# RWKV scan: the state product no longer waits for the copy of y from the other PSUM bank

## The chip, the cores and the metric

One core of one Trainium2 chip runs the whole program. The metric is the device time of one execution in microseconds; the number given for a kernel is the median over its runs.

## The reference

A decoder trunk of two layers on a sequence of 1024 tokens of width 1024, float32. Each layer normalises x, projects it with one wide input matrix and runs three token mixers beside each other: a pooling mixer, a retention mixer with 4 heads, and an RWKV-7 mixer with 8 heads of 64. Their outputs are gated, projected, merged by per-channel gates, projected once more and added to x. The part that matters here is the recurrence of RWKV-7, which carries a 64 x 64 state S for each head from token to token:

```
def step(S, inp):
    r_t, w_t, k_t, v_t, a_t, b_t = inp
    sa = einsum('bhvk,bhk->bhv', S, a_t)
    S = S * w_t[:, :, None, :] + sa[..., None] * b_t[:, :, None, :] + v_t[..., None] * k_t[:, :, None, :]
    return S, einsum('bhvk,bhk->bhv', S, r_t)
_, y = lax.scan(step, zeros, xs)
y = head_norm(y, RWKV_NORM_EPS) * ln_w + ln_b
```

## The kernel before, in words

**The wide work.** Everything that is a projection is done by one helper. The sequence lies along the free axis in two halves of 512 tokens. Every weight tile is split into a rounded part (wh, ScalarE) and a rest (wl, GpSimd), as are the activations (hhi and hlo), and three matmuls of 128 x 128 weights on 512 tokens (wh with hhi, wh with hlo, wl with hhi) stand for one exact product. They add up in one of three PSUM banks with the tag acc. A weight tile is 2 halves x 4 blocks x 3 products x 2 token halves = 48 such matmuls. This is what the groups acc<-hhi,wh, acc<-hhi,wl and acc<-hlo,wh in the profile are. `split` (L561 to L563) makes wh and wl, with three buffers for each.

**The side tasks.** The mixers are Python generators in lanes (norm, post, rwkv, mix, ada). After each three matmuls of the wide work, `pump` lets every lane advance whose due time has come on a clock that the kernel keeps by hand: `mmul` adds an estimate for each matmul, `settle` one for each operation of the other engines, and `wait(x)` gives the time until x is estimated to be there. So a step of a scan is spread between wide matmuls, and this fixes the order in which the program is written. In the first stretch (`manual_schedule`) this order is kept on the four compute engines. Behind it the compiler's list scheduler orders each engine's queue from that order and its own model of when an instruction's operands are ready, so an instruction that its model sees held back can be overtaken by later ones. The engines then run their queues in order.

**The scan.** `rwkv_task` handles two heads (128 channels) at a time, so there are four of them in a layer and eight in the program, one after the other. The tokens are taken in 16 chunks of 64. `prepare`, `scores`, `invert` and `states` make everything that doesn't depend on the state. Then the loop over c (L999 to L1042) does the following for each chunk:

- ScalarE scales the state with the chunk's decay into SP (L1007).
- TensorE multiplies the state with the chunk's rows of AR into cy (L1009). This is the **state product**, two<-S,AR in the profile. Rows 64 to 127 of its output go into the update, and rows 0 to 63 are the part of y that comes from the old state.
- VectorE adds AV and writes xst (L1010).
- Two small matmuls make ch from xst (L1016), VectorE copies it to Z (L1017), one matmul multiplies BKt with Z (L1019), and VectorE makes the new state of each head from that and SP (L1022, twice in a chunk, S in the profile).
- Two small matmuls add the chunk's own part onto rows 0 to 64 of cy (L1029, the **y products**, two<-Z,G in the profile).
- ScalarE copies rows 0 to 63 of cy to y (L1037, the **copy of y**).

A float32 matmul appears in the profile as two matmuls with two weight loads, so the y products of a chunk are four rows and the state product two.

**The shared tile.** cy is not a tile of its own. `two` is one PSUM tile of two banks, and `cyt()` hands out its halves in turn:

```
two = ps_c.tile([P, 2 * HF], F32, tag="two", name="two")
...
def cyt():
    turn[0] ^= 1
    return two[:, turn[0] * HF : (turn[0] + 1) * HF]
```

Two chunks that follow each other use different banks; chunk c and chunk c-2 use the same. Dependencies are found for the tile: the state product of chunk c, which writes one half, is held until the copy of y of chunk c-1 has read the other. `two` is also used by the preparation of the next pair of heads, for scores (L901), the inversion (L939, L945) and the small projections (L781).

Of the kernel before, what the change touches and what calls it, by code (L numbers as in the profile page):

```python
# [17 lines left out]
P = 128  # L18
# [78 lines left out]
def trunk_kernel(ctx, tc, xT, cvec, pos, vecs, consts, w_ada, w_all, pool_w, lora_w, out):  # L97
    nc = tc.nc
# [19 lines left out]
    def nm(s):  # L118
        uid[0] += 1
        return f"{s}_{uid[0]}"  # L120
# [24 lines left out]
    two = ps_c.tile([P, 2 * HF], F32, tag="two", name="two")  # L145
    turn = [0]
# [4 lines that stand above are left out]
# [4 lines left out]
    def r8(s):  # L155
        return rp.tile([P, 2048], F32, tag="r8", name=nm(s))
# [3 lines left out]
    o = CST["bone"]  # L160
# [175 lines left out]
    def settle():  # L336
        if seen[0] is None:
            return
        insts = nc.cur_bb.bb.instructions
        for j in range(seen[0], len(insts)):  # L340
            i = insts[j]
            e = i.engine
            if e not in idle_at and e != ET.PE and e != ET.SP:
                continue
            ins, outs = (
                [b for b in (getattr(x, "bass_ap", None) for x in y) if b is not None] for y in (i.ins, i.outs)
            )
            if not outs:
                continue
            t = max([ready.get(x.tensor.name, 0.0) for x in ins] + [0.0])  # L350
            base = t if any(x.space == PSUM for x in ins) else clock[0]
            if e == ET.PE:
                t = clock[0] + 280
            elif e != ET.SP:
                c = cost(i, e, ins, outs)
                idle_at[e] = max(idle_at[e], base) + c
                t = max(t + c, idle_at[e]) + 80
                for x in ins:
                    if x.space == PSUM:
                        ready[x.tensor.name] = max(ready.get(x.tensor.name, 0.0), t)  # L360
            for x in outs:
                ready[x.tensor.name] = t
        seen[0] = len(insts)

    def await_(out, *ins):
        names = [x.tensor.name for x in ins] + [behind.pop(out.tensor.name, "")]
        clock[0] = max(clock[0], *(ready.get(n, 0.0) for n in names))
# [14 lines left out]
    def wait(*aps, spare=0.0):  # L382
        settle()
        names = [x.tensor.name if hasattr(x, "tensor") else x.name for x in aps]
        t = max(ready.get(n, 0.0) for n in names) + spare
        if len(mxq) == 2:
            t = max(t, ready.get(mxq[0], 0.0) + 600)
        return max(0.0, t - clock[0])
# [43 lines left out]
    def add(k, task):  # L432
        if not lanes[k]:
            due[k] = clock[0]
        lanes[k].append(task)
        return task

    def mmul(out, lhsT, rhs, start=True, stop=True, timed=False, **kw):
        n = rhs.free_size()
        fast = rhs.dtype == F32R  # L440
        settle()
        await_(out, *(() if timed else (lhsT, rhs)))
        m = lhsT.free_size()
        clock[0] += (n + 32) / 2.4 if fast else 2 * max(n, 1.6 * m - 92, m - 16) * 0.875
        nc.tensor.matmul(out, lhsT=lhsT, rhs=rhs, start=start, stop=stop, **kw)  # L445

    def trans(out, in_, timed=False):
        settle()
# [99 lines left out]
    def mm1(ps, w, k, r, start, stop):  # L548
        (whi, wlo), (rh, rl) = w, r
        for j, (a, b) in enumerate(((whi, rh), (whi, rl), (wlo, rh))):  # L550
            mmul(ps, a[:, k * P : (k + 1) * P], b, start=(start and j == 0), stop=(stop and j == 2))
            pump()
# [139 lines left out]
    def layer_norm(y, n, w, eps, tile_, eng=nc.vector):  # L692
        y3 = y.rearrange("p (n w) -> p n w", w=w)
        mean = sp.tile([P, n], F32, tag="mn", name=nm("mn"))
        nc.vector.tensor_reduce(mean, y3, axis=mybir.AxisListType.X, op=ALU.add)
        nc.vector.tensor_scalar_mul(mean, mean, 1.0 / w)
        yc = tile_("yc")
        yc3 = yc.rearrange("p (n w) -> p n w", w=w)
        eng.tensor_tensor(
            yc3, y3, mean.unsqueeze(2).to_broadcast([P, n, w]), op=ALU.subtract  # L700
        )
        sq = tile_("ysq")
        nc.scalar.square(sq, yc)
        var = sp.tile([P, n], F32, tag="vr", name=nm("vr"))
        nc.vector.tensor_reduce(
            var, sq.rearrange("p (n w) -> p n w", w=w), axis=mybir.AxisListType.X, op=ALU.add
        )
        rsqrt(var, eps, 1.0 / w)
        eng.tensor_tensor(yc3, yc3, var.unsqueeze(2).to_broadcast([P, n, w]), op=ALU.mult)  # L709
        return yc  # L710
# [72 lines left out]
    def rwkv_task(l, hp, kT, rT, vp, lt, lw):  # L783
        hc = slice(hp * P, (hp + 1) * P)
        AR = r8("AR").rearrange("p (c j t) -> p c j t", j=2, t=CH)
# [11 lines left out]
        jt = lambda t, rows, c: t[rows, c, :, :].rearrange("p j t -> p (j t)")  # L797
# [118 lines left out]
        start = [0.0]  # L916
# [79 lines left out]
        for S in SS:  # L996
            nc.gpsimd.memset(S, 0.0)
        yield wait(MT, *SS)
        for c in range(16):  # L999
            par = c % 2  # L1000
            prog[(l, hp)] = c
            if c % 8 == 0:
                y = t_ri("y")
            S, Sn = SS[par], SS[1 - par]
            pcc = pc[:, c : c + 1]
            SP = sp.tile([P, P], F32, tag="SP", name=nm("SP"), bufs=1)
            nc.scalar.activation(SP, S, AF.Copy, scale=pcc)  # L1007
            cy = cyt()
            mmul(cy[:, 0:P], jt(AR, slice(0, P), c), S)  # L1009
            nc.vector.tensor_tensor(xst[0:64, :], cy[64:128, 0:P], AV[:, c * P : (c + 1) * P], op=ALU.add)  # L1010
            yield wait(xst)
            ch = ps_c.tile([P, HF], F32, tag="ch", name=nm("ch"))
            for hd in range(2):
                cols = slice(64 * hd, 64 * hd + 64)
                u0 = (16 * hd + c) * P
                mmul(ch[0:65, cols], Gf[:, u0 + 64 : u0 + 129], xst[:, cols])  # L1016
            nc.vector.tensor_copy(Z[0:64, c, :], ch[0:64, 0:P])  # L1017
            yield wait(Z)
            mmul(ch[:, P : 2 * P], BKt[:, c, :], Z[:, c, :])  # L1019
            for hd in range(2):  # L1020
                rw = slice(64 * hd, 64 * hd + 64)
                nc.vector.scalar_tensor_tensor(  # L1022
                    Sn[rw, rw], ch[rw, P + 64 * hd : P + 64 * hd + 64], pc[rw, c : c + 1], SP[rw, rw],
                    op0=ALU.mult, op1=ALU.add,
                )
            yield 500
            for hd in range(2):
                cols = slice(64 * hd, 64 * hd + 64)
                mmul(  # L1029
                    cy[0:65, cols],  # L1030
                    G[:, 16 * hd + c, 0:65],
                    Z[:, c, cols],
                    start=False,
                    skip_group_check=True,
                )
            o = (c % 8) // 2 * P
            nc.scalar.copy(y[64 * par : 64 * par + 64, o : o + P], cy[0:64, 0:P])  # L1037
            yield wait(Sn)
            if c % 8 == 7:
                h = c // 8  # L1040
                yn = layer_norm(y, 8, 64, RWKV_EPS, t_ri, nc.gpsimd)
                posts[l, hp, h] = add("post", rwkv_post(l, hp, h, yn, bvs[h]))  # L1042

    def rwkv_post(l, hp, h, yn, bv):
        yield 6500
        yield wait(yn, spare=3000)
        ps = mx("yt")
        for j in range(4):
            trans(ps[:, j * P : (j + 1) * P], yn[:, j * P : (j + 1) * P])
        ob = t_ri("wob")  # L1050
        nc.vector.scalar_tensor_tensor(ob, ps, vv(l, "ln_w", hp), bv, op0=ALU.mult, op1=ALU.add)
        nc.sync.dma_start(out=od[l][2, hp, h], in_=ob)
        yield 100
# [51 lines left out]
    def evac(item, ps, h):  # L1105
# [9 lines left out]
        elif kind in ("k", "r", "v"):  # L1115
# [8 lines left out]
            if kind == "v" and h == 1:  # L1124
                st[("task", i)] = rwkv_task(l, i, st[("k", i)], st[("r", i)], st[("v", i)], st["lt"], lw)
                add("rwkv", st[("task", i)])
# [279 lines left out]
    for l in range(L):  # L1406
# [94 lines left out]
        while wready[0][0][0] != "out":  # L1501
# [11 lines left out]
            else:  # L1513
# [6 lines left out]
                for d, h in dh:  # L1520
                    ps = acc_ps()
                    mm3(ps, ws[d - d0], [osplit[n][k][h] for k in range(4)], True, True)
                    o = (d % 2) * T + h * HF
# [28 lines left out]
        for part, (h, sl) in enumerate(parts):  # L1552
# [3 lines left out]
            for i, d in enumerate(out_order(l, part)):  # L1556
# [17 lines left out]
                for j in range(2):  # L1574
                    rhs = [[m[:, sl] for m in merged[k][h]] for k in range(4 * j, 4 * j + 4)]
# [129 lines left out]
```

## Time and profile before

| | us |
|---|---|
| runs | 2446.65, 2447.24, 2447.24 |
| median | 2447.24 |
| the profiled execution | 2443.31 |
| its span, first to last instruction | 2441.4 |
| mean granted clock of TensorE, share of full speed | 0.989 |
| TensorE busy | 2363.0 (97%) |
| VectorE busy | 1315.2 (54%) |
| GpSimd busy | 818.5 (34%) |
| ScalarE busy | 799.3 (33%) |

In the rows of the profile, PE is TensorE's matmuls, PEld its weight loads (which run beside the matmuls), DVE VectorE, ACT ScalarE, POOL GpSimd, SP SyncE, which issues the DMAs. "two<-S,AR" means that the tile two is written and S and AR are read. A row of the timeline gives the start in us from the begin of the span, the duration in us, engine, line and operation, and in brackets how long the engine had been idle and what ended that. L445 and L451 are the lines of the helpers through which all matmuls and transposes go, so they are told apart by their tiles. The ends of matmuls are modelled, their starts are recorded. In this trace the scans run in eight stretches, of which the first begins at 240 us and the last ends at 2099 us.

### The profile page before, as it was taken

The page shows a single profiled execution, that of the slowest core. Times are in us where ns is not written, and L with a number is a line of the kernel's source. Part 1 is how long each engine was busy: PE and PEld are TensorE (multiplying, and loading weights), DVE is VectorE, ACT ScalarE, POOL GpSimd, SP SyncE. Part 2 cuts the span into 40 slices and gives each one's busy share as a digit, 9 for nine tenths or more (in the row PEclk, how much of TensorE's full clock was granted, in tenths as well). Part 3 has the DMA queues.
Part 4 walks back from the last instruction along what each step waited for, and adds up shares of the span by engine and source line. Part 5 has one row for each costly group of instructions (what it writes and reads, how often), then busy time and mean ns, then how long its engine had stood idle before and what let it go on. Part 6 is the DMA issues. An engine that isn't in the chain of part 4 may idle for free. (4 is left out here: it accounts for less than half of the span.)

```text
span 2441.4 us, 34772 instructions
## 1 busy us (share of the span) xinstructions
PE 2363.0 (97%) x13312; PEld 1912.5 (78%) x13312; DVE 1315.2 (54%) x2564; ACT 799.3 (33%) x1481; POOL 818.5 (34%) x729
## 2 busy tenths in 40 slices
PE   5989999999999999999999999999999999999998
PEld 4768778778877878777877877887787888778888
DVE  7655477367458643457455646735644674322244
ACT  5542233333234222112354324323322322212243
POOL 4321232232232323374442222323313332455241
PEclk9999999999999999999999999999999999999999
DMA  7132112111213215666531211211111122543142
GB/s 251 49 109 70 40 40 75 44 48 46 70 54 109 75 61 165 191 211 194 162 118 44 79 40 40 80 39 44 63 61 40 62 75 73 183 129 97 54 151 79
DMA packets 122487, 220.52 MB, mean 90 GB/s; under 512 B 13904, under 2 KB 17232, under 8 KB 122320
## 3 DMA queue, kind: packets, MB, share of 16 engines
q1 hardware_dynamic: 122320, 218.29, 28.1%
q8 instruction: 105, 1.72, 0.3%
q14 instruction: 62, 0.51, 0.1%
HBM read 172.89 MB, written 45.35 MB: 89 GB/s over the span
## 5 line engine op out<-in xcount | busy, mean ns | idle before, releaser
L563 POOL TENSOR_TENSOR wl<-wr,wh 128x512 fp32r<-128x512 f32 x342 | 451.1, 1319 | 1161.1 <-ACT wh L562 1091.3
L445 PE MATMUL acc<-hhi,wh 128*128 128x512 f32 x2000 | 806.3, 403 | 7.8 <-ACT gsg L1140 6.6
L445 PE MATMUL acc<-hhi,wl 128*128 128x512 f32 x2000 | 809.2, 405 | 1.5 <-POOL r L1060 1.5
L445 PE MATMUL acc<-hlo,wh 128*128 128x512 f32 x2000 | 810.4, 405 | 0.0
L445 PEld LDWEIGHTS acc<-hhi,wh 128*128 128x128 f32 x2000 | 379.9, 190 | 76.3 <-ACT gsg L1140 7.9
L445 PEld LDWEIGHTS acc<-hhi,wl 128*128 128x128 f32 x2000 | 380.0, 190 | 67.9 <-POOL r L1060 2.0
L445 PEld LDWEIGHTS acc<-hlo,wh 128*128 128x128 f32 x2000 | 380.0, 190 | 64.7 <-issue 0.7
L562 ACT CAST wh<-wr 128x512 fp32r<-128x512 f32 x342 | 211.8, 620 | 629.6 <-PE acc L445 462.4
L445 PE MATMUL acc<-olo,wh 128*128 128x512 f32 x384 | 154.6, 404 | 5.9 <-POOL olo L563 5.9
L445 PE MATMUL acc<-oG,wh 128*128 128x512 f32 x384 | 154.3, 403 | 3.2 <-ACT oG L562 1.7
L445 PE MATMUL acc<-oG,wl 128*128 128x512 f32 x384 | 152.3, 398 | 0.0
L1010 DVE TENSOR_TENSOR xst<-two,MT 64x128 f32<-64x128 f32 x128 | 37.5, 293 | 182.2 <-PE two L445 181.4
L1022 DVE SCALAR_TENSOR_TENSOR S<-ch,pc,SP 64x64 f32<-64x64 f32 x256 | 72.5, 283 | 99.0 <-PE ch L445 96.2
L1007 ACT ACTIVATE SP<-S,pc 128x128 f32<-128x128 f32 x128 | 51.4, 402 | 213.1 <-DVE S L1022 202.8
L445 PEld LDWEIGHTS acc<-olo,wh 128*128 128x128 f32 x384 | 73.3, 191 | 24.8 <-POOL olo L563 8.6
L445 PEld LDWEIGHTS acc<-oG,wh 128*128 128x128 f32 x384 | 73.1, 191 | 23.3 <-ACT oG L562 2.9
L445 PEld LDWEIGHTS acc<-oG,wl 128*128 128x128 f32 x384 | 73.6, 192 | 17.6
L1529 DVE SCALAR_TENSOR_TENSOR gs<-gs,acc 128x512 f32<-128x512 f32 x64 | 43.5, 683 | 79.2 <-PE acc L445 79.2
L939 DVE TENSOR_TENSOR tm<-MT,two 64x30 f32<-64x30 f32 (+14 forms) x240 | 76.5, 319 | 12.9 <-ACT two L932 5.6
L945 DVE TENSOR_TENSOR two<-two,tm 64x30 f32<-64x30 f32 (+14 forms) x240 | 78.9, 329 | 7.3
L1527 DVE SCALAR_TENSOR_TENSOR mrg<-gs,acc 128x512 f32<-128x512 f32 x32 | 22.0, 686 | 107.6 <-PE acc L445 107.5
L1017 DVE COPY Z<-ch 64x128 f32<-64x128 f32 x128 | 36.0, 281 | 74.4 <-PE ch L445 73.9
(287 smaller groups left out, 3688.2 us busy)
## 6 DMA issues: line engine op xcount, KB each, us to landing
wr<-in_w_all SPq DMA_DIRECT2D x364, 256.0 KB, 2.6
gd<-gsg SPq DMA_DIRECT2D x74, 256.0 KB, 2.0
gs<-gd SPq DMA_DIRECT2D x74, 256.0 KB, 3.0
wada<-in_w_ada SPq DMA_DIRECT2D x70, 256.0 KB, 3.0
ol<-od SPq DMA_DIRECT2D x64, 256.0 KB, 2.9
ringG<-in_w_ada SPq DMA_DIRECT2D x26, 256.0 KB, 5.1
x<-in_xT SPq DMA_DIRECT2D x16, 256.0 KB, 4.9
od<-po SPq DMA_DIRECT2D x16, 256.0 KB, 2.0
```

The lines of the kernel that those rows point to most:

```text
L445: nc.tensor.matmul(out, lhsT=lhsT, rhs=rhs, start=start, stop=stop, **kw)
L562: nc.scalar.copy(hi, src)
L563: eng.tensor_tensor(lo, src, hi.bitcast(F32), op=ALU.subtract)
L939: nc.vector.tensor_tensor(pr, L3[:, i + 1 :, i : i + 1].to_broadcast([64, n, i]), M3[:, i : i + 1, 0:i].to_broadcast([64, n, i]), op=ALU.mult,
L945: nc.vector.tensor_tensor(M3[:, i + 1 :, 0:i], M3[:, i + 1 :, 0:i], pr, op=ALU.add)
L1007: nc.scalar.activation(SP, S, AF.Copy, scale=pcc)
L1010: nc.vector.tensor_tensor(xst[0:64, :], cy[64:128, 0:P], AV[:, c * P : (c + 1) * P], op=ALU.add)
L1017: nc.vector.tensor_copy(Z[0:64, c, :], ch[0:64, 0:P])
L1022: nc.vector.scalar_tensor_tensor(Sn[rw, rw], ch[rw, P + 64 * hd : P + 64 * hd + 64], pc[rw, c : c + 1], SP[rw, rw], op0=ALU.mult, op1=ALU.add,
L1527: nc.vector.scalar_tensor_tensor(m, s, 1.0, ps, op0=ALU.add, op1=ALU.mult)
L1529: nc.vector.scalar_tensor_tensor(s, s, 1.0, ps, op0=ALU.add, op1=ALU.mult)
```

## The change

`mmul` returns the instruction. The scan keeps the instructions of the copies of y in a list. For every chunk but the first it declares that the state product does not depend on the copy of the chunk before, and for every chunk from the third on it adds a dependency on the copy of the chunk before that, which read the same bank.

```diff
@@ mmul
-        nc.tensor.matmul(out, lhsT=lhsT, rhs=rhs, start=start, stop=stop, **kw)
+        return nc.tensor.matmul(out, lhsT=lhsT, rhs=rhs, start=start, stop=stop, **kw)
@@ rwkv_task
         yield wait(MT, *SS)
+        yout = []
         for c in range(16):
...
             cy = cyt()
-            mmul(cy[:, 0:P], jt(AR, slice(0, P), c), S)
+            sa = mmul(cy[:, 0:P], jt(AR, slice(0, P), c), S)
+            if c:
+                tc.declare_no_dep(sa.ins, yout[-1], reason="reads the other bank of two")
+            if c > 1:
+                tc.add_manual_dep(
+                    sa.ins,
+                    yout[-2].name,
+                    mybir.DependencyInfo(mybir.DependencyClass.Sync, mybir.DependencyReason.DATA),
+                    reason="read the same bank of two",
+                )
             nc.vector.tensor_tensor(xst[0:64, :], cy[64:128, 0:P], AV[:, c * P : (c + 1) * P], op=ALU.add)
...
             o = (c % 8) // 2 * P
-            nc.scalar.copy(y[64 * par : 64 * par + 64, o : o + P], cy[0:64, 0:P])
+            yout.append(nc.scalar.copy(y[64 * par : 64 * par + 64, o : o + P], cy[0:64, 0:P]).ins)
             yield wait(Sn)
```

## The prediction

> **What bounds the kernel now.** I read the page first: its busy times, its chain, its costliest group (behind the bar: busy time, mean ns of one, idle time before the group and what ended it).
>
> ```profile
> span 2441.4 us, 34772 instructions
> PE 2363.0 (97%) x13312; PEld 1912.5 (78%) x13312; DVE 1315.2 (54%) x2564; ACT 799.3 (33%) x1481; POOL 818.5 (34%) x729
> PE acc L445 13%; POOL olo L563 0%; PE ssps L445 0%; PE rbc L445 0%; DVE fin L627 0%; PE ch L445 0%; PE two L445 0%; DVE yc L709 0%; ACT wh L562 0%; POOL wl L563 0%; DVE xres L1577 0%; DVEq L1700 0%; DVE sq L1584 0%; PE yt L451 0%; PE rot L451 0%
> L445 PE MATMUL acc<-hhi,wh 128*128 128x512 f32 x2000 | 806.3, 403 | 7.8 <-ACT gsg L1140 6.6
> ```
>
> TensorE is busy 97% of the span, and what the chain could be followed through is nearly all wide matmuls into acc. What counts is how fast TensorE gets through its queue; a shorter chain of the scan is by itself worth nothing. Next, the busy time in the eight stretches in which the scan of one pair of heads runs (16 chunks each):
>
> ```profile
> core 0: us, PE busy (x) PEld busy (x) DVE busy (x) ACT busy (x) POOL busy (x), PEclk, DMA share, GB/s
> sum 604.00, PE 600.27 PEld 476.34 DVE 266.89 ACT 164.15 POOL 167.01; mean PE 75.03 PEld 59.54 DVE 33.36 ACT 20.52 POOL 20.88
> ```
>
> TensorE looks full there, 600 of 604 us. But the ends of matmuls are modelled, and a stretched matmul counts as busy, so time lost must be looked for in the starts. The waits of the weight loads, totals over the run, name a place:
>
> ```profile
> engine line waited for: us in total, times, longest us
> PEld two L445 <- ACT y L1037: 35.2, 98, 0.6
> PEld ch L445 <- DVE Z L1017: 8.9, 14, 1.7
> ```
>
> 98 of the 128 state products (two<-S,AR) load their weights late, behind the copy of y. The timeline shows one of them, an even chunk, in the order of time:
>
> ```profile
> 247.32 0.29 DVE L1022 SCALAR_TENSOR_TENSOR S<-ch,pc,SP 64x64 f32<-64x64 f32 x1
> 247.52 0.39 PE L445 MATMUL two<-Z,G 128*65 128x64 f32 x4
> 247.70 0.40 ACT L1007 ACTIVATE SP<-S,pc 128x128 f32<-128x128 f32 x1 [0.30 <-DVE S L1022]
> 247.72 0.48 PE L445 MATMUL acc<-hlo,wh 128*128 128x512 f32 x1
> 248.04 0.40 PE L445 MATMUL acc<-hhi,wl 128*128 128x512 f32 x1
> 248.13 0.26 ACT L1037 COPY y<-two 64x128 f32<-64x128 f32 x1
> 248.44 0.30 PEld L445 LDWEIGHTS two<-S,AR 128*128 128x128 f32 x2 [0.44 <-ACT y L1037]
> 248.44 0.49 PE L445 MATMUL two<-S,AR 128*128 128x128 f32 x2
> 248.69 0.48 PE L445 MATMUL acc<-hhi,wh 128*128 128x512 f32 x1
> ```
>
> The y products (two<-Z,G) are queued first, then two wide matmuls, then the state product. S was complete at 247.32 + 0.29 = 247.61. The copy of y ran behind the scaling of S on ScalarE and ended at 248.39, and the weights were loaded at 248.44, 0.05 later. An odd chunk, where the copy does not queue behind the scaling, and one in which the copy (at 252.07) was long done:
>
> ```profile
> 269.80 0.29 DVE L1022 SCALAR_TENSOR_TENSOR S<-ch,pc,SP 64x64 f32<-64x64 f32 x1
> 270.49 0.24 ACT L1037 COPY y<-two 64x128 f32<-64x128 f32 x1
> 270.51 0.40 PE L445 MATMUL acc<-hlo,wh 128*128 128x512 f32 x1
> 270.78 0.30 PEld L445 LDWEIGHTS two<-S,AR 128*128 128x128 f32 x2 [0.31 <-ACT y L1037]
> 271.03 0.47 PE L445 MATMUL acc<-hhi,wl 128*128 128x512 f32 x1
> ...
> 252.07 0.24 ACT L1037 COPY y<-two 64x128 f32<-64x128 f32 x1
> 252.57 0.39 PE L445 MATMUL acc<-hlo,wh 128*128 128x512 f32 x1
> 252.80 0.40 PE L445 MATMUL acc<-hhi,wl 128*128 128x512 f32 x1
> 252.80 0.42 PEld L445 LDWEIGHTS two<-S,AR 128*128 128x128 f32 x2
> 253.03 0.38 PE L445 MATMUL two<-S,AR 128*128 128x128 f32 x2
> 253.17 0.48 PE L445 MATMUL acc<-hhi,wh 128*128 128x512 f32 x1
> ```
>
> From the wide matmul before the state product to the one behind it takes 0.65 us in the even chunk (248.04 to 248.69), 0.52 in the odd one and 0.37 in the free one. So the waits cost TensorE 0.28 and 0.15 us, and each is 0.16 less than the idle time of the weight loads beside it (0.44, 0.31): the load is normally issued with the matmul ahead, and a start up to 0.16 late costs nothing.
>
> **The change part by part.** *Removed:* the wait of the state product of chunk c for the copy of chunk c-1. By the rows, 98 waits of 35.2 us in all, less 98 × 0.16 = 15.7 us that lay under the matmul ahead, are 19.5 us of TensorE. A few of the 98 only bear the copy's name, and in them S was late:
>
> ```profile
> 861.30 0.58 DVE L1022 SCALAR_TENSOR_TENSOR S<-ch,pc,SP 64x64 f32<-64x64 f32 x2
> 861.57 0.26 ACT L1037 COPY y<-two 64x128 f32<-64x128 f32 x1 [3.65 <-PE two L445]
> 861.66 0.40 PE L445 MATMUL acc<-hhi,wh 128*128 128x512 f32 x1
> 862.00 0.30 PEld L445 LDWEIGHTS two<-S,AR 128*128 128x128 f32 x2 [0.38 <-ACT y L1037]
> 862.25 0.48 PE L445 MATMUL acc<-hlo,wh 128*128 128x512 f32 x1
> ...
> 1843.32 0.30 PEld L445 LDWEIGHTS two<-S,AR 128*128 128x128 f32 x2 [0.39 <-ACT y L1037]
> ```
>
> Here the copy ended at 861.83, S at 861.88, and the load came 0.12 behind S: that is the shortest way from S to the load. The interval is 0.59, so 0.22 is lost and stays lost. There are four such (these are the first and the last): 0.9 us off, which leaves 18.6 us.
>
> *What is late next.* In the even chunk S would have let the load start at 247.61 + 0.12 = 247.73, and the latest start without loss is 248.04 + 0.16 = 248.20: 0.47 us to spare. In the odd one it is 270.21 against 270.67: 0.46. A wide matmul takes 0.23 (252.57 to 252.80), so S does not take the copy's place unless the product moves up by more than two of them.
>
> *Moved.* The queue of TensorE is ordered when the kernel is compiled, from a model of what is ready. With the edge to the copy gone, that model may put the state product one wide matmul earlier. In the ordinary chunk this costs nothing (0.23 of the 0.46 is used). Where S comes late, a product moved up waits for S by as much as 0.23: in the four above, 0.9 us, and over all chunks ten products that have S under about 0.35 us ahead of the load (or more steps to go up) give 3.5 us together; the first and the last of the ten:
>
> ```profile
> 310.14 0.30 PEld L445 LDWEIGHTS two<-S,AR 128*128 128x128 f32 x2 [0.26 <-ACT y L1037]
> ...
> 2086.93 0.30 PEld L445 LDWEIGHTS two<-S,AR 128*128 128x128 f32 x2 [0.83 <-issue]
> ```
>
> So the gain is 18.6 us with the order kept and 15.1 with all products moved up. I take 17, between them, because the model that moves a product also sees S as late in some of these chunks.
>
> *Added:* a wait for the copy of chunk c-2, which ended a whole chunk ago (the copies at 248.13 and 252.07 stand 3.94 apart). Its cover is a chunk long; as an instruction of its own on TensorE's queue it would at most cost some hundredths of a microsecond behind a matmul that runs for 0.23. I take nothing; above, 128 × 0.05 (the step from the copy's end to the load) = 6.4 us; below nothing, since a wait can't gain. The later readers and writers of the tile (xst, the y products, the next preparation) keep their edges.
>
> *Who must keep up.* A faster TensorE asks earlier for split weights. ScalarE waits for TensorE with that, not the other way round:
>
> ```profile
> ACT wh L562 <- PE acc L445: 462.4, 182, 5.9
> DVE xst L1010 <- PE two L445: 181.4, 102, 19.4
> ```
>
> The casts wait 462 us in all for wh buffers that matmuls still read, so 17 us are there; and xst waits for the state product, and would come earlier with it, so the distance in the queue from the state product to the ch products is not shortened. If that cover were gone, TensorE would idle before acc, which it now does for 7.8 us in the largest group.
>
> *Sum.* The profiled execution took 2443.31 us, its span 2441.4. 2443.3 − 17 = 2426.3 for such an execution. The median of the runs is 2447.24, 3.9 above the profiled one; less 17 it is 2430.2. About 0.2% (5 us) is what a measurement of this kernel can tell from no change.
>
> [...] The overlap of weight loads decides how much of the 35.2 us counts. At 252.80 the load of the state product starts together with a wide matmul of all 128 rows and is 0.42 long for two, so it runs under that matmul. [...]
>
> **The rivals.** (a) *All idle time of the weight loads counts.* For it: the waits are listed as idle time. Against: the three intervals above. 2447.2 − 35.2 = 2412.0. Faster.
>
> (b) *S takes the copy's place.* If the product goes up past both wide matmuls and the four y products (247.52 to 247.72: 0.20), it is asked for 0.66 us earlier, and waits 0.66 − 0.47 = 0.19 in each of 120 chunks (all but the first of each scan): 23 us, in place of 18.6. Time 2451, no change that can be told. Half-way forms, where S or a late DVE takes a part, give a gain of 5 to 14 us, 2433 to 2442. Against the full form: the y products read Z, which is there before S.
>
> (c) *Nothing is removed.* Another edge (the whole tile is one name; xst and the y products use it too) still ties the load to the copy: loads stay 0.05 behind it. 2447.
>
> (d) *Slower: xst goes ahead of evacuations on VectorE.* VectorE runs in queue order. If the model, which now sees the state product earlier, puts xst ahead of an operation that empties an acc bank, then on the chip that operation waits with xst; xst's mean wait is already 181.4 / 102 = 1.8 us. It decides from the point where an acc bank is given back later than TensorE needs it. With some 600 / 11 = 55 weight tiles in the scans (a tile is 48 wide matmuls of 0.23, 11 us) and one evacuation (0.75, the row below) late in each, 41 us would be lost against 18 gained: 2470. Against: TensorE hardly waits for acc banks now (7.8 us above).
>
> ```profile
> 247.64 0.75 DVE L1066 SCALAR_TENSOR_TENSOR k<-acc,omu,k 128x512 f32<-128x512 f32 x1
> ```
>
> **How the numbers follow.** The forecast (gain 15 to 20 us) 0.72; half-way forms of (b) 0.10; (a) 0.03; (c) with the full form of (b) 0.09; (d) 0.06. Faster by over 0.2%: 0.72 + 0.10 + 0.03 = 0.85; within: 0.09; slower: 0.06. The time is the forecast's, 2430. The range runs from 2423, a gain of 18.6 with the 5 us of measurement on top, to 2442, which takes in the half-way forms and the 6.4 us of an added wait; outside stay (a), (c) and (d), 0.18. The forecast's own range is 2427 to 2432.
>
> **What would show it.** Right: the row "PEld two <- ACT y" all but gone; the interval across a state product 0.37 in nearly all chunks; the load no longer 0.05 behind the copy but issued with the matmul ahead; the scan stretches some 2 us shorter each, and the rest as long as before. The move would be seen as one wide matmul between y products and state product in place of two. Wrong: loads that start 0.12 behind S (b), 0.05 behind a copy (c), idle time of TensorE before acc with VectorE as releaser (d).

## The result, and the profile after

The changed kernel takes 2432.15 us (median of 4 runs, 2431.49 to 2433.14); the kernel before, run beside it, takes 2446.94 (2446.14 to 2447.24). The ratio is 0.994, 95% interval 0.9923 to 0.9958: 14.8 us faster, where 17 were predicted. The time lies in the predicted range of 2423 to 2442 and just outside the narrower 2427 to 2432 of the forecast. The profiled execution took 2433.14 us.

From the page of the changed kernel, its span, its busy times and the first group of matmuls:

```profile
span 2431.3 us, 34768 instructions
PE 2353.2 (97%) x13312; PEld 1925.5 (79%) x13312; DVE 1313.5 (54%) x2564; ACT 799.9 (33%) x1481; POOL 820.8 (34%) x729
L445 PE MATMUL acc<-hhi,wh 128*128 128x512 f32 x2000 | 808.6, 404 | 9.6 <-ACT gsg L1150 8.2
```

TensorE is as full as before, 97%, and its work is the same in number; the idle time ahead of the wide matmuls has hardly grown (7.8 to 9.6 us in the first group). The waits of the weight loads, the longest first ("..." stands for rows left out):

```profile
engine line waited for: us in total, times, longest us
PEld ssps L445 <- DVE sq L1211: 14.9, 2, 11.6
...
PEld ch L445 <- DVE Z L1027: 7.8, 12, 1.4
...
PEld two L445 <- DVE S L1032: 3.0, 9, 0.9
```

The row that led the list, 35.2 us behind the copy of y, is gone. Nine products now bear the name of S, 3.0 us together. What an ordinary chunk looks like, in the timeline (this is the odd chunk that the prediction showed at 269.80 to 271.03):

```profile
270.00 0.58 DVE L1032 SCALAR_TENSOR_TENSOR S<-ch,pc,SP 64x64 f32<-64x64 f32 x2 [1.40 <-PE ch L445]
270.49 0.40 PE L445 MATMUL two<-Z,G 128*65 128x64 f32 x4
270.69 0.48 PE L445 MATMUL acc<-hhi,wh 128*128 128x512 f32 x1
270.77 0.43 PEld L445 LDWEIGHTS two<-S,AR 128*128 128x128 f32 x2
270.98 0.24 ACT L1047 COPY y<-two 64x128 f32<-64x128 f32 x1
271.01 0.38 PE L445 MATMUL two<-S,AR 128*128 128x128 f32 x2
271.15 0.47 PE L445 MATMUL acc<-hlo,wh 128*128 128x512 f32 x1
271.46 0.39 PE L445 MATMUL acc<-hhi,wl 128*128 128x512 f32 x1
```

The load of the state product starts at 270.77, under the wide matmul of 270.69 and 0.21 before the copy of y has even begun. And one wide matmul stands between the y products and the state product, where there were two: the queue's order moved it up.

How long the scans take, from the wide matmul ahead of the first state product to the sixth behind the last, so that the same wide matmuls bound each stretch in both kernels. First two of the eight stretches of the kernel before and the sum of all, then the same of the changed kernel:

```profile
core 0: us, PE busy (x) PEld busy (x) DVE busy (x) ACT busy (x) POOL busy (x), PEclk, DMA share, GB/s
439.74:511.11 71.37, 70.68 (x414) 55.34 (x413) 29.74 (x81) 19.24 (x49) 19.12 (x20) 1.00 0.15 45
2012.51:2096.18 83.67, 82.21 (x509) 67.15 (x508) 41.30 (x103) 23.05 (x54) 20.15 (x16) 1.00 0.22 73
sum 600.74, PE 597.01 PEld 473.68 DVE 265.79 ACT 163.57 POOL 166.72; mean PE 74.63 PEld 59.21 DVE 33.22 ACT 20.45 POOL 20.84
```

```profile
core 0: us, PE busy (x) PEld busy (x) DVE busy (x) ACT busy (x) POOL busy (x), PEclk, DMA share, GB/s
436.44:505.63 69.19, 68.33 (x415) 56.45 (x413) 29.73 (x81) 19.24 (x49) 19.45 (x20) 1.00 0.15 45
2003.83:2086.38 82.55, 81.07 (x510) 68.42 (x509) 41.07 (x103) 23.02 (x54) 19.98 (x16) 0.99 0.24 74
sum 584.38, PE 580.52 PEld 481.43 DVE 265.93 ACT 163.70 POOL 167.53; mean PE 72.57 PEld 60.18 DVE 33.24 ACT 20.46 POOL 20.94
```

The scans are 600.74 − 584.38 = 16.4 us shorter: 1.85, 2.18, 2.55, 2.07, 2.28, 2.17, 2.14 and, in the last, 1.12 us. The span is only 10.1 us shorter (2441.4 to 2431.3), so the stretches outside the scans grew by 6.3 us in this pair of profiles. The granted clock goes with that. Its mean over the profiled execution is 0.985, after 0.989 before, so by the clock TensorE lost some 27 us in the profiled execution of before and some 37 us in this one, 10 us more and nearly all of it outside the scans. In most of the nine stretches outside the scans the growth follows the clock: the one between the fourth and the fifth scan is 3.7 us longer with 3.4 us more lost, the one between the fifth and the sixth unchanged with nothing more lost. The profiled execution of before had a high clock for this kernel: the mean over 52 of its runs is 0.9862.

Since the clock changes from run to run, I set span against clock over the runs of the kernels in the table, with one slope for all: each 0.001 of clock costs 1.6 us (what remains scatters by 1.6 us). That is two thirds of the 2.4 us which 0.001 of the span would be, so the 10 us lost above stand for some 7 us of time, close to the 6.3. The slope gives for each kernel a span at clock 0.986, used beside the medians (one execution of e3, at a clock of 0.557 and 3839.86 us, is left out everywhere):

| kernel | runs | mean clock | span at clock 0.986, us |
|---|---|---|---|
| before | 52 | 0.9862 | 2447.6 |
| changed (with e1) | 8 | 0.9851 | 2428.7 |
| e2: no wait, order of before | 6 | 0.9848 | 2431.1 |
| e3, e6: no wait in even chunks | 9, 8 | 0.9847, 0.9842 | 2438.9, 2437.6 |
| e4: no wait in odd chunks | 10 | 0.9857 | 2442.0 |
| e5: as before, edge without effect | 8 | 0.9876 | 2446.3 |
| e8: layer norm behind Z | 12 | 0.9858 | 2441.0 |

At equal clock the change is worth 2447.6 − 2428.7 = 18.9 us by this estimate. The pair of profiles alone gives less: 10.1 us of span and some 7 for the clock.

### The profile page after: what moved, and what is told of

Read it like the earlier page. It is cut to its first block, busy times and chain, and to the rows that moved or that the text cites. A ratio compares the mean times of both kernels' runs of the same rounds, so it can differ in the third digit from the quotient of the medians.

```text
span 2431.3 us, 34768 instructions
## 1 busy us (share of the span) xinstructions
PE 2353.2 (97%) x13312; PEld 1925.5 (79%) x13312; DVE 1313.5 (54%) x2564; ACT 799.9 (33%) x1481; POOL 820.8 (34%) x729
## 5 line engine op out<-in xcount | busy, mean ns | idle before, releaser
L1020 DVE TENSOR_TENSOR xst<-two,MT 64x128 f32<-64x128 f32 x128 | 37.6, 293 | 157.8 <-PE two L445 143.8
```

## The experiments

**e1: the changed kernel again**, unedited. The expectations of e1 to e4 bound a scan otherwise than the windows above, from its first state product to its last: by that measure the eight scans take 584.4 us before and 567.2 in the changed kernel. That the windows above also give 584.38, for the changed kernel, is chance.

> The changed kernel once more, for the clock and the spread beside the runs below. Theory (the stretches outside the scans differ only by the granted clock): 2432 us, give or take 3, with scan stretches that sum to 567 us as in its first profile, and a clock of 0.985. Rival (the change itself disturbs the stretches outside the scans): the same stretches are longer again by the same amounts as in its first profile, whatever the clock.

2431.96 us (2427.54 to 2434.75), ratio 0.9926, 0.9903 to 0.9948. The scans are 15.8 us shorter than before in its profile, 567.4 us by the expectation's measure, at a clock of 0.984. The gain comes again, and so does the rest: outside the scans e1 is 7.3 us longer than before, with half clock in nearly the same stretches as the changed kernel's first profile. As its clock is low too, this doesn't part the theory from its rival.

**e2: without the wait, in the order of before.** The change does two things: the wait goes, and most products stand one wide matmul earlier. Here the changed kernel holds each product behind one more wide matmul by an edge of order alone (this and the later edits are shortened, and their comments are added here):

```
+        if fast and n == HF:
+            while held:
+                tc.add_manual_dep(held.pop(), ins.ins.name, <NoSync>, ...)
...
             sa = mmul(cy[:, 0:P], jt(AR, slice(0, P), c), S)
             if c:
+                held.append(sa.ins)
```

> The wait for the copy is gone as in the changed kernel, but each state product is held (in the queue's order alone) behind one more wide matmul, which is where the kernel before had it. Theory A (only the wait counts, the place in the queue is free): the interval across an ordinary state product is 0.37 us, the eight scan stretches sum to 584.4 - 18.5 = 566 us, the time is within 3 us of the changed kernel (2429 to 2435). Rival B (the gain comes from the product standing one matmul earlier, which shortens the chain of a chunk): half of the gain or more is lost, scan stretches 575 us or more, time 2440 or more.

2434.95 us (2431.14 to 2438.08), ratio 0.9943, 0.9926 to 0.996. The interval across the product is 0.373 us in the ordinary chunk, the free one of the prediction, and the scans are 14.9 us shorter, with 1.8 us more lost to the clock inside them. 96 of its products stand two wide matmuls behind the y products, where 85 of before did. So the removed wait brings the gain without the move. It is the wait and not the instruction that waited: the free chunk of the prediction (252.80) carried the instruction too (51 ns, at 251.71) and took the same 0.37. Where the late product shows is the next step of the scan, in the waits of e2:

```profile
PEld ch L445 <- DVE xst L1032: 20.3, 96, 0.6
```

The loads of the ch products now start late behind xst, 20.3 / 96 = 0.21 us each. Most of it is covered, as it was with the copy: the interval across the ch products is 0.456 us in the mean against 0.447 in the changed kernel.

**e3, e4, e6: the wait taken from every other chunk.** e3 and e6 are one kernel; e4 is its mirror image with `c % 2`:

```
-            if c:
+            if c and c % 2 == 0:
                 tc.declare_no_dep(sa.ins, yout[-1], ...)
-            if c > 1:
+            if c > 1 and c % 2 == 0:
```

> The wait is taken from the even chunks alone. Theory A (a wait costs its idle time less 0.16 us): the even chunks had 43 waits of 0.27 us, so the scan stretches become 11 us shorter than before's 584.4, 573; the odd chunks keep 0.13 to 0.15 each. Time 2436. Rival C (each removed wait is worth the same, as a fixed cost of waiting): 43 of 96 waits give 8.3 us, 576, and the odd chunks' intervals stay as they are in either case.

> The wait is taken from the odd chunks alone. Theory A: 53 waits of 0.14 us, the scan stretches become 7.5 us shorter than before's 584.4, 577; time 2440. Rival C (a fixed cost of each wait): 53 of 96 waits give 10.2 us, 574, more than the even chunks give.

> The wait for the copy of the chunk before is taken away in the even chunks alone, and kept in the odd ones, as in e3, whose profile came from a chip at little over half clock and can't be set beside the others. Theory A (each chunk's wait pays by itself): the scans are 8 to 11 us shorter than before when the same wide matmuls are set beside each other, which with the 6.2 us of the odd chunks alone gives about the 16.4 us of both; the row of load idle time behind the copy is left with some 48 waits of the odd chunks; 2436 to 2441 us. Rival B (the waits are coupled: what one chunk saves its neighbour waits for): scans 2 to 5 us shorter, 2443 to 2446 us, and the waits left are longer than 0.36 us each.

e3: 2443.14 us (nine runs), ratio 0.9976 (0.9963 to 0.9989); it has no profile that can be used. e6: 2441.93, ratio 0.9977 (0.9965 to 0.9989). e4: 2443.37, ratio 0.998 (0.9966 to 0.9995). The waits that are left, e4 first, then e6:

```profile
PEld two L445 <- ACT y L1047: 19.3, 47, 0.5
```

```profile
PEld two L445 <- ACT y L1047: 15.7, 51, 0.5
```

e4 keeps the long waits of the even chunks (19.3 / 47 = 0.41 us each), e6 the short ones of the odd (0.31). They add up to 35.0, the 35.2 of before: a wait taken from one chunk doesn't reappear in its neighbour. By the same wide matmuls the scans are 8.5 us shorter in e6 and 6.2 in e4, together 14.7 of the 16.4 of both (1.7 us more was lost to the clock inside e6's scans). Each chunk's wait pays by itself. The even chunks bring more, since their copy queues behind the scaling of S on ScalarE (in the rows of before the scaling starts at 247.70 and takes 0.40, the copy starts at 248.13). So Rival C of e3 and e4, a fixed cost of each wait, falls: the odd chunks have more waits (51 against 47) and bring less. Both medians of this kernel lie above the times put down for Theory A (2436, and 2436 to 2441), with a clock below that of the kernel before; at equal clock the spans are 8.7 and 10 us below it.

**e5, e10: the earlier place with the wait kept.** e5 gave the next matmul that is written after the product an edge of order behind it:

```
+            ahead.append(mmul(cy[:, 0:P], jt(AR, slice(0, P), c), S).ins)
```

> The kernel before with its wait for the copy of y kept, and only the place of the state product changed: it is put one wide matmul (0.23 us) earlier, behind the first wide matmul after the y products, the place in which most products of the changed kernel stand. Theory A (what pays is the wait that is gone, the earlier place alone pays nothing): the load now begins its wait for the copy 0.23 us sooner and ends it at the same time, so each of the 98 waits grows by up to 0.23 us, the row of load idle time behind the copy rises from 35.2 to 52 to 58 us, the interval across the product from 0.57 to 0.66 us to 0.80 to 0.88 us, and the kernel takes 2462 to 2470 us. Rival B (the earlier place is what pays, and the copy could be waited for anywhere): 2432 to 2440 us, the row stays near 35 us.

2445.76 us, ratio 0.9987 (0.9972 to 1.0002): no change, since the edit did not move the product. In its trace two or three wide matmuls still stand between the y products and the product; the scheduler had filled the place with other wide matmuls. e10 holds the wide matmuls between back as well:

```
+            if c and len(wide) < 5:       # wide: those since the y products
+                for w in wide[1:]:
+                    after_S(w)            # order alone: w behind the product
```

> What e5 was meant to be; in e5 the product still stood two or three wide matmuls behind the y products. Here the kernel before keeps its wait for the copy of y, and the wide matmuls between are held behind the product: in the queue's order 53 products stand one wide matmul after the y products (before: 3), 40 two, 13 three; some hundred other matmuls also change places. Theory A (the earlier place pays nothing without the wait's going): in the 53 chunks the wait grows by 0.23 us, 12 us in all, the row of load idle time behind the copy rises from 35.2 to 43 to 48 us, and the kernel takes 2454 to 2462 us. Rival B (the earlier place pays by itself): 2436 to 2443 us. Rival C (the later wide matmul covers a later wait, so that the place makes no difference): 2445 to 2450 us.

2469.51 us, ratio 1.0094 (1.0076 to 1.0112); scans 20.5 us longer than before. An even chunk of e10:

```profile
258.54 0.48 PE L445 MATMUL acc<-hhi,wl 128*128 128x512 f32 x1
258.93 0.26 ACT L1059 COPY y<-two 64x128 f32<-64x128 f32 x1
259.24 0.30 PEld L445 LDWEIGHTS two<-S,AR 128*128 128x128 f32 x2 [0.54 <-ACT y L1059]
259.49 0.47 PE L445 MATMUL acc<-hhi,wh 128*128 128x512 f32 x1
```

The last line is the wide matmul behind the product, and the interval is 258.54 to 259.49 = 0.95 us, where before it was 0.65. The two can't be set beside each other as they are, since here the wide matmul ahead of the product is the one directly behind the y products, whose own step is longer (0.32 us in place of 0.23). From that one on, three steps take 1.49 us in e10 (258.54 to 260.03) and 1.28 before (247.72 to 249.00): the earlier place lost 0.21 us in this chunk, near the 0.23 of Theory A. But the row of waits, 35.6 us in 95 times, is as large as before, and not the 43 to 48 that I expected:

```profile
PEld two L445 <- ACT y L1059: 35.6, 95, 0.7
```

Over the scans, the 98 products of e10 with wide matmuls alone on both sides take 0.622 us in the mean against 0.534 of before, 8.6 us together, of which some 2 are the longer step just named. The rest isn't divided: the edges also threw other small matmuls (lw and yt) beside products, where 10 intervals with lw and 6 with yt in them take 21 us in all, part of it work that stood elsewhere before, and 2.8 us more is lost to the clock inside the scans. So Theory A holds in sign, with a time above its 2454 to 2462, and B and C fall, but the loss isn't a clean price of the place. What can be said is that the earlier place pays nothing as long as the wait is there.

The same traces tell why the row of waits did not grow with the loss. What a late load costs is the interval less that of a product that does not wait (0.37, or 0.46 directly behind the y products). In before, 100 late loads stand behind a second or later wide matmul, and in each of them 0.16 to 0.17 us of the idle time is covered. In e10, 24 stand directly behind the first one, and there 0.05 is covered.

**e8, e9: the layer norm in VectorE's queue.** In three scans the step behind chunk 7 gained nothing. Chunk 8 of the first scan, before and after, ScalarE's square being the last step ahead of these rows:

```profile
277.94 0.69 DVE L705 TENSOR_REDUCE vr<-ysq 128x8 f32<-128x512 f32 x1 [1.89 <-ACT ysq L703]
278.66 0.28 DVE L1017 COPY Z<-ch 64x128 f32<-64x128 f32 x1
278.99 0.30 PEld L445 LDWEIGHTS ch<-Z,BKt 128*128 128x128 f32 x2 [1.01 <-DVE Z L1017]
```

```profile
278.10 0.39 PE L445 MATMUL acc<-hlo,wh 128*128 128x512 f32 x1
278.29 0.69 DVE L705 TENSOR_REDUCE vr<-ysq 128x8 f32<-128x512 f32 x1 [1.89 <-ACT ysq L703]
279.00 0.28 DVE L1027 COPY Z<-ch 64x128 f32<-64x128 f32 x1
279.34 0.30 PEld L445 LDWEIGHTS ch<-Z,BKt 128*128 128x128 f32 x2 [1.28 <-DVE Z L1027]
279.58 0.48 PE L445 MATMUL acc<-hhi,wl 128*128 128x512 f32 x1
```

Z stands in VectorE's queue behind the layer norm's second reduce, which waits for a chain of copy, mean, difference and square. That chain starts at the y products of chunk 7, ahead of the removed wait, so it didn't move up against them, and TensorE reaches the load of ch<-Z sooner only to wait 1.28 instead of 1.01 us. VectorE did not take Z out of the queue's order: in before the last matmul into ch had ended at 277.04 + 0.40 = 277.44, VectorE was idle until the reduce at 277.94, and Z ran behind it, at 278.66. e8 puts both reduces of the layer norm between chunks 7 and 9 behind Z:

```
+            if late:                       # the two reduces, one per chunk
+                tc.add_manual_dep(late.pop(0), zc.ins.name, <NoSync>, ...)
```

> The changed kernel with the two reduces of the layer norm between chunks 7 and 9 put behind the copy Z of the next chunks on VectorE (the sum of y behind Z of chunk 8, the sum of squares behind Z of chunk 9), where they stood ahead of xst and Z of chunk 8. Theory A (in chunk 8 of scans 0, 1 and 3 VectorE's queue took a part of what the removed wait saved: the interval across ch<-Z,BKt grew there from 1.21, 1.21 and 0.99 us to 1.48, 1.49 and 1.09 us): these three intervals fall to 0.37 to 0.5 us, these scans are 0.6 to 1.1 us shorter each, in all 2 to 3 us, and the time is 2428 to 2431 us. Rival B (TensorE's own order or the state S holds chunk 8, not the layer norm): the three intervals stay above 1 us, 2431 to 2434 us. Rival C (the layer norm is then late for its transposes yt or the queue of VectorE is late for S): waits of yt for yc or of the products for S appear, 2433 to 2438 us.

2442.35 us, ratio 0.9974 (0.9959 to 0.9989): faster than before, 10 us slower than the changed kernel. The cause was named rightly: no load waits at that place any more.

```profile
278.53 0.28 DVE L1032 COPY Z<-ch 64x128 f32<-64x128 f32 x1 [1.96 <-PE ch L445]
278.84 0.69 DVE L695 TENSOR_REDUCE mn<-y 128x8 f32<-128x512 f32 x1
```

But the same profile has a new row near the top of its waits:

```profile
PEld yt L451 <- POOL yc L713: 14.6, 8, 2.4
```

Eight times the transposes yt, whose place in TensorE's queue stayed, wait up to 2.4 us for the normed y; in the changed kernel the idle time ahead of all 64 of these loads is 2.0 us. It was Rival C in kind, with a time above its 2433 to 2438. By the intervals between wide matmuls, those with yt in them take 24.7 us where they took 11.9 in the changed kernel, 12.8 us paid for 2.9 saved in chunk 8. e9 also moves the task with the transposes later:

```
-        yield 6500
+        yield 6500 if h else 10500
```

> As e8 (the two reduces of the layer norm between chunks 7 and 9 behind Z of chunks 8 and 9), and the task that transposes the normed y is put 10500 in place of 6500 behind the layer norm in the planner's time. In e8 the three intervals of chunk 8 fell from 1.48, 1.49 and 1.09 us to under 0.47 us, but the loads of the transposes yt then waited 14.6 us for yc, eight times, where they wait 2.0 us in the changed kernel. Theory A (those waits are the whole of what e8 lost): yt waits under 3 us, the three intervals stay under 0.5 us, and the time is 2427 to 2431 us, below the changed kernel's. Rival B (the later task is late for something else, such as the last products or the DMA of its result, or the planner's new order costs as much): 2431 to 2440 us.

2458.22 us, ratio 1.0052 (1.0039 to 1.0066), slower than before. The whole order of the program shifts with that number: yt still waits for yc seven times, 10.3 us, and other waits grew (nps for ksl to 8.3 us from 4.4). Rival B, and more than it said; part of it is a low clock (0.982 in the mean of its five runs). No version tried here beats the changed kernel.

**e7, e11: what the half clock follows.** Seven of the stretches at half clock in the changed kernel's profile begin behind the inversion's bursts of 32x32 matmuls. The first of them, in the timeline and in three windows of 6.8 us:

```profile
229.36 2.21 PE L445 MATMUL m<-MT,G 32*32 32x32 f32 x64
...
232.16 2.57 PE L445 MATMUL m<-G,MT 32*32 32x32 f32 x64
234.66 0.80 PE L445 MATMUL acc<-hlo,wh 128*128 128x512 f32 x1
235.25 0.63 PE L445 MATMUL acc<-hhi,wl 128*128 128x512 f32 x1
235.68 0.63 PE L445 MATMUL acc<-hhi,wh 128*128 128x512 f32 x1
```

```profile
core 0: us, PE busy (x) PEld busy (x) DVE busy (x) ACT busy (x) POOL busy (x), PEclk, DMA share, GB/s
226.90:233.70 6.80, 6.80 (x126) 5.69 (x125) 0.00 (x0) 2.06 (x4) 0.00 (x0) 1.00 0.24 80
233.70:240.50 6.80, 6.80 (x36) 5.48 (x33) 0.00 (x0) 1.96 (x4) 1.28 (x1) 0.50 0.23 77
240.50:247.30 6.80, 6.80 (x42) 5.67 (x41) 1.50 (x6) 1.20 (x3) 1.29 (x1) 1.00 0.02 9
```

The wide matmuls stand 0.43 us apart there (235.25 to 235.68) instead of 0.23, though TensorE counts as busy throughout (6.80 of 6.80 us). e7 cuts the bursts into groups of four, by a `yield 1` after every fourth product:

> The changed kernel with the bursts of 32x32 matmuls of the inversion (m<-MT,G and m<-G,MT, 64 in a row) cut into groups of four with wide matmuls between, same work. In the profile of the changed kernel 7 of the 14 stretches at half clock, 37 us of them (18.7 us lost), begin right behind such a burst. Theory A (the burst, in which the wide array does little, is what brings the half clock behind it): those stretches are gone or fewer than three, the mean granted clock rises from 0.985 to 0.990 to 0.993, and the time falls to 2414 to 2424 us. Rival B (the half clock comes by itself, whatever ran before): 0.984 to 0.986, as many stretches elsewhere, 2429 to 2435 us. Rival C (groups put between wide matmuls cost more loads and switches than they save): 2436 to 2445 us at an unchanged clock.

2514.29 us, ratio 1.0268 (1.0249 to 1.0286), and the clock of its profile is 0.966. None of the three had it. The inversion's products now take 14 to 16 us in each head pair instead of 4.7 to 6.7, and half clock holds for up to 17.1 us there; 3.4 to 8.5 us is lost at each of the eight places, 55 us in all where the changed kernel loses 19. That is less than half of the 82 us by which e7 is slower than the changed kernel; the rest was not traced to a cause. e11 goes the other way, with one product of 32x512 for each 16:

```
-            for u in range(16):
-                uu = 16 * q + u
-                mmul(ps[32:64, u * 32 : u * 32 + 32], G[0:32, uu, 96:128], T13[:, uu, :], timed=True)
+            mmul(ps[32:64, :], G[0:32, 16 * q, 96:128], T13[:, 16 * q : 16 * q + 16, :], timed=True)
```

> The changed kernel with each row of 16 products of 32x32 in the inversion replaced by one product 32x512 of the first block, so the inversion's values are not those of the reference; TensorE's bursts of 64 short matmuls (2.2 and 2.6 us, one behind the other) become four short single ones. e7, which cut the bursts into groups with wide matmuls between, made the stretches at half clock longer, not rarer. Theory A (wide array little used for some microseconds is what brings half clock behind it, and e7 only stretched that time): the stretches behind m are gone, clock 0.990 to 0.994, and with the matmuls left out (some 4 us for each of 8 heads) the time is 2380 to 2400 us. Rival B (half clock comes at that place for another reason, such as the wide matmuls setting in again after the two layers' changes of tiles): the stretches stay, clock 0.984 to 0.987, 2400 to 2415 us.

2416.49 us (2412.93 and 2420.05), at a clock of 0.991 in its profile. Of the stretches behind the inversion one is left, 3.4 us long. The clock is the one that Theory A put down (0.990 to 0.994). Its time was missed (2380 to 2400), because the matmuls were hardly shorter for being fewer. The same products in e11, in the first pair of heads:

```profile
230.93 1.90 PE L445 MATMUL m<-MT,G 32*32 32x512 f32 x4
233.66 1.90 PE L445 MATMUL m<-G,MT 32*32 32x512 f32 x4
```

The four long products take 1.90 us where the 64 short ones took 2.21 and 2.57. Over the run the intervals with these products in them fall from 42.9 to 36.7 us, 6.2 us where Theory A had counted on some 32. So the half clock at this place goes with the bursts of short matmuls: with them left out it is nearly gone (3.4 us left), and with them spread over nearly three times the time (e7) it is longer (up to 17.1 us). It does not go with the 32x32 weights as such, which e11 still uses for 3.8 us. Whether the number of the matmuls, their length or the unbroken time brings it is not shown.

## Why the prediction was right

*The removed wait: 98 × 0.16 off 35.2 us.* Right. e2, which removes the wait and keeps the order, has the free interval of 0.37. The intervals across its products fall by 67.3 − 49.4 = 17.9 us, where 18.6 were put down for the kept order. Its scans fall by 14.9, or 16.7 with the 1.8 lost to the clock. The two halves of e4 and e6 add up. The 0.16 was read off two chunks, but it holds in all of the 100 loads counted under e10. That a weight load runs under a wide matmul of all 128 rows is seen in the changed kernel too: the load at 270.77 is 0.43 long and begins 0.08 behind the wide matmul of 270.69, and the state product itself starts at 271.01.

*The move.* "May put the state product one wide matmul earlier": it did: 91 products stand one wide matmul behind the y products, where before 3 did, and 85 stood at two. "In the ordinary chunk this costs nothing" was right in the sum. The interval across the product is 0.46 and not the 0.37 that I named as the sign, but the wide matmul directly behind the y products takes 0.31 or 0.32 in any case (247.72 to 248.04 in the rows of before), and it now is the same one. From the y products on, e2 has 0.31 + 0.37 + 0.31, the changed kernel 0.46 (270.69 to 271.15) + 0.31 + 0.23: 0.99 and 1.00. The sum over the intervals says the same: across the product 67.3 us before, 55.9 after, 49.4 in e2; between wide matmuls with nothing between, 352.4, 346.1 and 353.5.

*S late.* Bounded at 0.9 to 3.5 us. Nine products wait for S, 3.0 us of idle time; less 0.16 each it is 1.6 us, and the intervals across them give the same. The slack of 0.46 us held: one step up uses half of it, and rival (b) did not come. The shortest way from S to the load, 0.12 by the row of 861.30, is now shorter: here S ends at 475.29 and the load comes 0.06 later. That the second wait, which is gone, made the difference is likely but not tested.

```profile
474.72 0.57 DVE L1032 SCALAR_TENSOR_TENSOR S<-ch,pc,SP 64x64 f32<-64x64 f32 x2
475.35 0.34 PEld L445 LDWEIGHTS two<-S,AR 128*128 128x128 f32 x2
```

*The added wait, taken at nothing.* Right: no row of the waits names it, and in the traces the instructions for matmuls that only wait (51 ns each) fell from 261 to 141, so it came with the product itself. What I had not listed: xst got a second wait, 112 short instructions of some 21 ns on VectorE, at a place where VectorE sits idle (143.8 us in all ahead of 88 of the 128, until the state product).

*What is late next.* The half-way form, "a late DVE takes a part", came in small: in chunk 8 of three scans the interval across ch<-Z grew by 0.27, 0.28 and 0.10 us, shown by e8 to be the layer norm's doing. That is 0.65 of the 2.2 us by which the scans fall short of 18.6; half clock at the start of the last scan, the one that gained least, and the 0.7 us that the late S cost beyond the 0.9 already taken off are others.

*The rivals.* (a) would have given 2412, and 16.4 of the 35.2 us came back in the scans. (c) falls with the row of waits. (d) did not come: the loads of acc wait 3.4 us for VectorE, before 5.2.

*The sum.* Predicted 17 of 15.1 to 18.6; the scans gave 16.4, the medians 14.8, and the runs at equal clock 18.9. What failed is "the rest as long as before": the rest is 6.3 us longer in the profile, by half clock. The step left out is that the median of 2447.24 and the profiled 2443.31 differ by the clock, and that the clock of the changed kernel could differ as well: its mean is 0.9851 against 0.9862, 1.8 us at 1.6 us for each 0.001. That this shift left the time near the forecast is in part luck, since single runs of the kernel before lie between 0.981 and 0.990. Whether the change itself brings the lower clock stays open: e1 has it in the same stretches, and the variants in the table lie at 0.9842 to 0.9876.

## What to carry to other kernels

Price a wait on TensorE by the interval between the wide matmuls on both sides of it, not by the idle time of the weight load: some 0.16 us of that was covered here, and where the product stood directly behind the first wide matmul only 0.05. Before moving a step off a wait, ask which engine's queue is late next and how far its chain starts ahead of the wait. And an operation put later (e8) is paid by whoever waits for it at a place that doesn't move: 12.8 us for 2.9 there.

## What the runs showed of the hardware

In the changed kernel's profile TensorE's granted clock halves (1.00 to 0.50) for 3.4 or 6.8 us at a time behind the inversion's 128 matmuls of 32x32 (some 5 us with the wide ones between) in seven of the eight head pairs, in that of before in six of the eight. TensorE is busy for the whole of each of these stretches and of the 6.8 us ahead of it (6.80 of 6.80 us in the windows 226.90:233.70, at a clock of 1.00, and 233.70:240.50, at 0.50). These stretches hold 19 of the 37 us that the changed kernel loses by the clock, and 14 of the 27 us of before. Stretching the short matmuls over 14 to 16 us brought the clock to 0.966, putting long ones in their place to 0.991.
